# A two-layer decoder trunk: Relu and square of the MLP's partial sums emitted later than the sum, transposes spaced by bank

## The chip, the core and the metric

The kernel runs on one core of a Trainium2 chip. Five engines work side by side, each through its own list of instructions: TensorE (PE in the profile, with its weight loads as PEld), VectorE (DVE), ScalarE (ACT), GpSimd (POOL) and SyncE (SP, which here only issues transfers). The metric is the device time of one execution in microseconds (us); less is better.

## The reference

One sequence of 256 tokens with 1024 features passes two layers. Each adds a mixer (retention in layer 0, block attention in layer 1) and then an MLP, both between RMS norms. All is float32.

```
def sq_relu_mlp(x, w_up, w_down):
    h = jax.nn.relu(x @ w_up)
    return (h * h) @ w_down
...
    for i in range(DEPTH):
        pre, post, w_in, w_out, mpre, mpost, w_up, w_down = layers[i]
        h = h + rms_norm(mixers[i % N_MIXERS](rms_norm(h, pre), w_in, w_out), post)
        h = h + rms_norm(sq_relu_mlp(rms_norm(h, mpre), w_up, w_down), mpost)
```

`w_up` is 1024 x 4096 and `w_down` 4096 x 1024 in each layer; `w_in` is 1024 x 6144 in layer 0 and 1024 x 3072 in layer 1.

## The kernel before

**Numbers in two halves.** Every operand of a matmul is split into a high half in a faster float format and the rest: ScalarE copies it to `whi` (L181), VectorE subtracts to get `wlo` (L182), and TensorE makes three matmuls for each product, high x high (L238), high x low and low x high (L239, L240). Activations go the same way (L257 and L258, called `split`, tiles `act` and `qkT`). So each weight tile of 128 x 1024 costs one ScalarE instruction, one VectorE instruction and its transfer.

**The stream of weights.** `Stream` loads the weights through SP into four buffers `raw` and, for `w_up`, into four larger tiles `quad`, and turns them into `whi` and `wlo`, of which there are ten. When the next tile is split is decided as the program is written out: `Flow.now` is a clock in us that each matmul moves on by a fixed amount, and `Stream.split` may not come again before `next_t`, which it moves on by a `cost` (L172 to L176). The same clock orders the rest: a step written as a generator (`flow.spawn`) goes on when the delay that it yielded is over. These numbers only fix the order of each engine's list; on the chip the engines wait for one another by semaphores.

**The up projection.** The 4096 hidden features are eight groups of 512, and the 256 tokens two tiles `t` of 128. Groups 0 and 1 are made plainly (`in_groups_skewed`). Groups 2 to 7 come in three blocks of two groups, in a 2 x 2 scheme with seven products of half size where eight would be plain (`up_blocks`). The weight sums of the scheme are made in place in the `quad` tiles, by VectorE (L187) or by a transfer that GpSimd issues and that adds (L191). The products accumulate in three PSUM tiles, `px`, `py` and `pz`. After each product `down()` makes one step of the down projection of the two groups before (`dn`), so that TensorE goes back and forth between them. A block ends in four partial sums, each of which is squared:

- the first `pz` plus `u3` (group g+1, tile 1), after the second `py` product;
- `px` alone (group g, tile 0);
- `py` plus `p1` (group g, tile 1);
- the last `pz` plus `u2` (group g+1, tile 0), at the end of the block.

`squared` (L473) adds on VectorE (`c`, L479), applies Relu on ScalarE (L480, or L477 where nothing is added) and squares on ScalarE (L481). `turned` (L465) then waits its delay and has TensorE transpose `c` with four 128 x 128 transposes into a PSUM tile `tp_u`, which `split` brings to the hidden tile `act` for the down projection of the next block.

**PSUM.** `px`, `py`, `pz` and the transposes' tiles come from a pool of four banks. In layer 1 the last accumulator of the down projection (`dn_4961` in the order) holds one of the four, so three are left.

**The mixers.** In layer 1 `prep` copies a sum of q or k (`yq`, ScalarE), rotates it on GpSimd (`ropea`, `yq`, L860 to L865), waits its delay and has it transposed (`tp_q`). In layer 0 the first head's scores (`sd`, L740) are split to `sds` and used by the matmuls `o`.

Of the kernel before, what the change touches and what calls it, by code (L numbers as in the profile page):

```python
# [13 lines left out]
AF = mybir.ActivationFunctionType  # L14
# [3 lines left out]
P = 128  # L18
# [85 lines left out]
class Stream:  # L104
# [57 lines left out]
    def split(self, pres=(None,)):  # L162
        nc = self.nc
        while self.loaded() is None:
            assert self.load()
        op = self.order.pop(0)
        hi = self.pool.tile([P, CH], F32R, tag="whi", name="whi", bufs=self.slots)
        lo = self.pool.tile([P, CH], F32R, tag="wlo", name="wlo", bufs=self.slots)
        full = len(self.ready) >= (6 if self.quads else 4)
        if op is None:  # L170
            raw = self.raw.pop(0)[0]
            cost = (1.5 if self.quads else 2.0) if full else 1.2  # L172
        else:
            raw = self.quads[op.q][:, op.half, :]
            cost = 1.5 if full else 1.2
        n = len(pres)  # L176
        for i, pre in enumerate(pres):
            c = slice(i * CH // n, (i + 1) * CH // n)
            if pre:
                pre()  # L180
            nc.scalar.activation(hi[:, c], raw[:, c], AF.Copy)  # L181
            nc.vector.tensor_sub(lo[:, c], raw[:, c], hi[:, c].bitcast(F32))  # L182
        if op is not None:
            for q, add, name in op.sums:
                o, a = self.quads[q][:, op.half, :], self.quads[add][:, op.half, :]
                if name[1] in ("u1", "u2"):
                    nc.vector.tensor_add(o, o, a)  # L187
                    cost += 1.1
                    self.landed[name] = 0.0
                else:  # L190
                    nc.gpsimd.dma_start(o, a, accum_op=ALU.add)  # L191
                    self.dma_t = max(self.dma_t, self.flow.now) + 2.8
                    self.landed[name] = self.flow.now + 7.0
        self.live += 1
        self.quad_ops += op is not None
        self.ready.append(Chunk(hi, lo, CH * S if op is None else CH * P))
        self.next_t = max(self.next_t, self.flow.now) + cost
        while len(self.raw) < self.raws and self.load():
            pass
# [23 lines left out]
def body(ctx, tc, xT, x, gT, gpost, w_in_0, w_out_0, w_up_0, w_down_0, w_in_1, w_out_1, w_up_1, w_down_1,  # L223
# [50 lines left out]
    def new_e2(shape, name):  # L274
        return work.tile(shape, F32, tag="e2", name=name, bufs=6)
# [160 lines left out]
    def in_groups_skewed(hT, then, ready=None):  # L436

        held = []
        hT.ready(0)
        for g in range(2):  # L440
            held.append([])
            o = new_acc("ip")
            for c in range(4):
                held[g].append(ws.get())
                in_tile(hT, held[g][c], c, 0, o)
            then(g, 0, o)
        hT.ready(1)
        if ready:
            ready()
        for g in range(2):  # L450
            o = new_acc("ip")
            for c in range(4):
                in_tile(hT, held[g][c], c, 1, o)
            then(g, 1, o)


    def mlp(hT, gain, nxt, gi, qpool):
# [4 lines left out]
        def new_hid(g):  # L462
            hid[g] = new_act().rearrange("p (u j s) -> p u j s", u=2, j=4)

        def turned(g, t, c, delay):  # L465

            yield delay
            tp = new_ps([P, 4, P], "tp_u")
            turn4(tp, c)
            ts = slice(t * P, (t + 1) * P)  # L470
            split(hid[g][:, 0, :, ts], hid[g][:, 1, :, ts], tp)

        def squared(g, t, o, add=None, sign=1.0, delay=4.6):  # L473

            c = new_e2([P, 512], "c")
            if add is None:
                nc.scalar.activation(c, o, AF.Relu, scale=sign)  # L477
            else:
                nc.vector.tensor_add(c, o, add)  # L479
                nc.scalar.activation(c, c, AF.Relu, scale=sign)  # L480
            nc.scalar.activation(c, c, AF.Square)  # L481
            done[g].append(flow.spawn(turned(g, t, c, delay)))

        s_hi, s_lo = [p.tile([P, 4, 4, P], F32R, name=n, tag="act" if p is act else n)
                      for p, n in ((act, "s_hi"), (qpool, "s_lo"))]
# [33 lines left out]
        def up_blocks(g, down):  # L519


            x = new_ps([P, 512], "px")
            product(x, quad(0, 0), True)
            p1 = new_e2([P, 512], "p1")
            nc.scalar.activation(p1, x, AF.Copy)
            down()
            flow.finish(*sums)
            z = new_ps([P, 512], "pz")
            product(z, hsum(0), True)
            down()  # L530
            y = new_ps([P, 512], "py")
            product(y, hsum(1), True)
            u2 = new_e2([P, 512], "u2")
            nc.vector.tensor_add(u2, y, p1)
            down()
            product(y, hsum(2), False)
            u3 = new_e2([P, 512], "u3")
            nc.vector.tensor_add(u3, y, p1)
            squared(g + 1, 1, z, u3, -1.0, 8.0)
            down()  # L540
            product(x, quad(0, 1), False)
            squared(g, 0, x)
            down()
            product(y, quad(1, 1), False)
            squared(g, 1, y, p1)
            down()
            product(z, hsum(3), False)
            squared(g + 1, 0, z, u2, -1.0)
            down()
            down()  # L550

        def lhs(k, t):
# [4 lines left out]
        new_hid(0)  # L557
        new_hid(1)
        sums = []
        in_groups_skewed(hT, lambda g, t, o: squared(g, t, o, delay=3.6),  # L560
                         lambda: sums.append(flow.spawn(block_sums(), 1.0)))
        gb = load_gain(gain)
        rs2 = []
# [282 lines left out]
    def prep(qk, u, t, ps, wait):  # L846

        scale = hT.rs[t]
        if u == 0:
            if rsq[t] is None:  # L850
                rsq[t] = small_t("rsq")
                nc.gpsimd.tensor_scalar(rsq[t], hT.rs[t], float(MDH) ** -0.5, None, op0=ALU.mult)
            scale = rsq[t]
        y = new_e2([P, HH, MDH], "yq")
        nc.scalar.activation(y.rearrange("p h d -> p (h d)"), ps, AF.Copy, scale=scale)
        a = new_e2([P, 4, HH, 16], "ropea")
        cosb = cr[:, 0, t, None, :].to_broadcast([P, HH, 16])
        sinb = cr[:, 1, t, None, :].to_broadcast([P, HH, 16])
        x1, x2 = y[:, :, 0:16], y[:, :, 16:32]
        nc.gpsimd.tensor_mul(a[:, 0], x1, cosb)  # L860
        nc.gpsimd.tensor_mul(a[:, 1], x2, sinb)
        nc.gpsimd.tensor_mul(a[:, 2], x2, cosb)
        nc.gpsimd.tensor_mul(a[:, 3], x1, sinb)
        nc.gpsimd.tensor_sub(x1, a[:, 0], a[:, 1])
        nc.gpsimd.tensor_add(x2, a[:, 2], a[:, 3])  # L865
        yield wait
        tp = new_ps([P, HH, P], "tp_q")
        turn4(tp, y.rearrange("p h d -> p (h d)"))
        ts = slice(t * P, (t + 1) * P)
        split(qk[:, 0, :, ts], qk[:, 1, :, ts], tp)  # L870
# [112 lines left out]
    v, pts, rsq = [None, None], [], [None, None]  # L983
    qk = [new_qk(u) for u in range(2)]
    pq = []
    in_groups_skewed(hT, lambda g, t, o: pq.append(flow.spawn(prep(qk[g], g, t, o, 4.4))))
    gb = load_gain(2)
    first = flow.spawn(heads0(qk, pq))
    qk1 = [new_act().rearrange("p (a h s) -> p a h s", a=2, h=HH) for u in range(2)]
# [117 lines left out]
```

## Time and profile before

| | |
|---|---|
| time, median of 3 runs | 697.04 us (696.73 to 697.16) |
| time of the profiled execution | 697.66 us |
| its span, first to last instruction | 695.9 us |
| TensorE busy | 672.2 us, 97% of the span |
| VectorE busy | 492.6 us, 71% |
| ScalarE busy | 408.9 us, 59% |
| GpSimd busy | 101.6 us, 15% |
| read from memory | 123.39 MB, 179 GB/s over the span |

Busy is the time in which an engine has at least one instruction running. Matmuls overlap, and the profile models their ends. A time such as 275.46 is us from the start of the span. A bracket such as [3.38 <-ACT c L481] at the end of a row says how long the engine stood idle ahead of it, and which instruction ended that wait.

### The profile page before, as it was taken

What the parts mean: (1) busy time and instruction counts of PE and PEld (TensorE: products, weight loads), DVE (VectorE), ACT (ScalarE), POOL (GpSimd) and SP (SyncE); (2) the same over time, 40 slices, a digit from 0 to 9 for tenths busy, and PEclk for the clock granted to TensorE, in tenths of its full rate; (3) what the DMA queues carried; (4) which work ended last, traced back from release to release, by engine and by line L of the source; (5) the groups of instructions that cost most, each with busy time, mean ns of one, the idle gap of its engine ahead of it and who ended that gap; (6) DMA issues with size and microseconds to landing.
All of it is one profiled execution on the core that took longest, in us unless ns stands there. A gap on an engine that the chain in (4) does not pass through costs nothing.

```text
span 695.9 us, 9115 instructions
## 1 busy us (share of the span) xinstructions
PE 672.2 (97%) x3367; PEld 563.9 (81%) x3367; DVE 492.6 (71%) x595; ACT 408.9 (59%) x575; POOL 101.6 (15%) x162
## 2 busy tenths in 40 slices
PE   8999999999999998998999999999999989989996
PEld 6879898988888886786888878888888868878885
DVE  5578765666466978877866867776669777778643
ACT  6476645446355855755575657665558557555741
POOL 0122120211001100101100163912011000001001
PEclk9999999999999999999999999999999999999998
DMA  8767645464737597695647557533375976856411
GB/s 274 278 211 269 223 151 190 156 208 151 240 126 302 129 350 217 172 331 129 181 152 243 175 161 259 178 122 122 142 289 138 345 215 168 334 123 182 152 61 61
DMA packets 39645, 137.62 MB, mean 198 GB/s; under 512 B 4656, under 2 KB 5168, under 8 KB 39600
## 3 DMA queue, kind: packets, MB, share of 16 engines
q1 hardware_dynamic: 36144, 124.45, 51.1%
q0 software_dynamic: 3456, 12.58, 10.3%
q8 instruction: 26, 0.43, 0.2%
q14 instruction: 19, 0.16, 0.1%
HBM read 123.39 MB, written 1.05 MB: 179 GB/s over the span
## 4 chain that ended last, share of the span: by engine, by line
PE 69%; DVE 12%; ACT 8%; issue 5%; POOL 3%; DMA 2%; SPq 0%; POOLq 0%; DVEq 0%; ACTq 0%
PE ip L238 7%; PE ip L240 7%; PE ip L239 7%; DVE wlo L182 6%; PE dn L240 5%; PE dn L239 5%; PE dn L238 5%; ACT whi L181 4%; PE out L238 3%; PE out L240 3%; PE out L239 3%; PE qk L238 2%; PE qk L240 2%; PE qk L239 2%; DMA quad<-quad 1%
## 5 line engine op out<-in xcount | busy, mean ns | idle before, releaser
L182 DVE TENSOR_TENSOR wlo<-raw,whi 128x1024 fp32r<-128x1024 f32 (+1 forms) x179 | 213.6, 1207 | 86.1 <-ACT whi L181 78.1
L181 ACT ACTIVATE whi<-raw 128x1024 fp32r<-128x1024 f32 (+1 forms) x179 | 182.1, 1037 | 33.7 <-PE out L240 10.9
L182 DVE TENSOR_TENSOR wlo<-quad,whi 128x1024 fp32r<-128x1024 f32 x84 | 100.2, 1219 | 23.1 <-ACT whi L181 23.1
L238 PE MATMUL ip<-whi,act 128*128 128x512 f32 x288 | 114.2, 397 | 0.0
L239 PE MATMUL ip<-wlo,act 128*128 128x512 f32 x288 | 112.5, 390 | 0.2 <-DVE wlo L182 0.2
L240 PE MATMUL ip<-whi,act 128*128 128x512 f32 x288 | 112.4, 390 | 0.0
L238 PE MATMUL dn<-whi,act 128*128 128x512 f32 (+1 forms) x288 | 106.5, 370 | 0.0
L240 PE MATMUL dn<-whi,act 128*128 128x512 f32 (+1 forms) x288 | 105.6, 367 | 0.0
L239 PE MATMUL dn<-wlo,act 128*128 128x512 f32 (+1 forms) x288 | 105.3, 366 | 0.0
L181 ACT ACTIVATE whi<-quad 128x1024 fp32r<-128x1024 f32 x84 | 86.4, 1049 | 21.8 <-DMA quad<-quad 15.2
L240 PEld LDWEIGHTS ip<-whi,act 128*128 128x128 f32 x288 | 54.1, 188 | 11.6
L239 PEld LDWEIGHTS ip<-wlo,act 128*128 128x128 f32 x288 | 54.2, 188 | 10.7 <-DVE wlo L182 0.7
L238 PEld LDWEIGHTS ip<-whi,act 128*128 128x128 f32 x288 | 54.1, 188 | 10.0
L240 PEld LDWEIGHTS dn<-whi,act 128*128 128x128 f32 x288 | 54.2, 188 | 9.8 <-DVE act L258 0.9
L239 PEld LDWEIGHTS dn<-wlo,act 128*128 128x128 f32 x288 | 54.3, 188 | 9.4
L238 PEld LDWEIGHTS dn<-whi,act 128*128 128x128 f32 x288 | 54.3, 188 | 9.2
L191 POOL DMA_DIRECT2D quad<-quad x24 | 21.2, 882 | 206.2 <-DVE quad L187 100.2
L480 ACT ACTIVATE c<-c 128x512 f32<-128x512 f32 x18 | 11.4, 632 | 66.9 <-DVE c L479 66.9
L238 PE MATMUL qk<-act,whi 128*128 128x256 f32 x128 | 37.8, 296 | 1.4 <-ACT whi L181 1.4
L238 PE MATMUL out<-whi,act 128*128 128x512 f32 x96 | 37.8, 394 | 0.0
L240 PE MATMUL qk<-act,wlo 128*128 128x256 f32 x128 | 37.6, 293 | 0.0
L240 PE MATMUL out<-whi,act 128*128 128x512 f32 x96 | 37.4, 390 | 0.0
(187 smaller groups left out, 1116.1 us busy)
## 6 DMA issues: line engine op xcount, KB each, us to landing
raw<-in_w_in SPq DMA_DIRECT2D x69, 512.0 KB, 4.4
raw<-in_w_down SPq DMA_DIRECT2D x64, 512.0 KB, 5.0
quad<-in_w_up SPq DMA_DIRECT2D x48, 512.0 KB, 7.7
raw<-in_w_out SPq DMA_DIRECT2D x24, 512.0 KB, 3.4
quad<-quad POOLq DMA_DIRECT2D x24, 512.0 KB, 5.4
raw<-in_w_up SPq DMA_DIRECT2D x16, 512.0 KB, 3.6
gb<-in_gpost SPq DMA_DIRECT2D x4, 512.0 KB, 7.9
raw<-in_w_in SPq DMA_DIRECT2D x6, 256.0 KB, 5.9
```

The source lines that it names most:

```text
L181: nc.scalar.activation(hi[:, c], raw[:, c], AF.Copy)
L182: nc.vector.tensor_sub(lo[:, c], raw[:, c], hi[:, c].bitcast(F32))
L191: nc.gpsimd.dma_start(o, a, accum_op=ALU.add)
L238: nc.tensor.matmul(o, a[0], b[0], start=first, stop=False, skip_group_check=again)
L239: nc.tensor.matmul(o, a[0], b[1], start=False, stop=False, skip_group_check=again)
L240: nc.tensor.matmul(o, a[1], b[0], start=False, stop=last, skip_group_check=again)
L480: nc.scalar.activation(c, c, AF.Relu, scale=sign)
```

## The change

`turned` and `squared` become one generator. It allocates `c`, adds where there is something to add, and then yields 2.2 us of the program's clock before it writes out Relu and square; where there is nothing to add, Relu and square follow at once, as they did. The delays ahead of the transposes are new: 4.0 instead of 4.6, to which the 2.2 come, for the third and the fourth sum, 6.0 instead of 8.0 plus the 2.2 for the first, 6.5 instead of 4.6 for the sum without an add. The first two groups keep 3.6. The first four transposes of q and k wait 5.6 instead of 4.4. And the `cost` of a split outside the up projection is 1.3 instead of 1.2 while few tiles are ready.

```diff
@@ -169,7 +169,7 @@
-            cost = (1.5 if self.quads else 2.0) if full else 1.2
+            cost = (1.5 if full else 1.2) if self.quads else (2.0 if full else 1.3)
@@ -462,24 +462,23 @@
-        def turned(g, t, c, delay):
-
+        def squared(g, t, o, add=None, sign=1.0, delay=4.0):
+
+            c = new_e2([P, 512], "c")
+            if add is not None:
+                nc.vector.tensor_add(c, o, add)
+                yield 2.2
+                o = c
+            nc.scalar.activation(c, o, AF.Relu, scale=sign)
+            nc.scalar.activation(c, c, AF.Square)
             yield delay
             tp = new_ps([P, 4, P], "tp_u")
             turn4(tp, c)
             ts = slice(t * P, (t + 1) * P)
             split(hid[g][:, 0, :, ts], hid[g][:, 1, :, ts], tp)
 
-        def squared(g, t, o, add=None, sign=1.0, delay=4.6):
-
-            c = new_e2([P, 512], "c")
-            if add is None:
-                nc.scalar.activation(c, o, AF.Relu, scale=sign)
-            else:
-                nc.vector.tensor_add(c, o, add)
-                nc.scalar.activation(c, c, AF.Relu, scale=sign)
-            nc.scalar.activation(c, c, AF.Square)
-            done[g].append(flow.spawn(turned(g, t, c, delay)))
+        def square(g, *args):
+            done[g].append(flow.spawn(squared(g, *args)))
@@ -536,16 +535,16 @@
-            squared(g + 1, 1, z, u3, -1.0, 8.0)
+            square(g + 1, 1, z, u3, -1.0, 6.0)
...
-            squared(g, 0, x)
+            square(g, 0, x, None, 1.0, 6.5)
...
-            squared(g, 1, y, p1)
+            square(g, 1, y, p1)
...
-            squared(g + 1, 0, z, u2, -1.0)
+            square(g + 1, 0, z, u2, -1.0)
@@ -983,7 +982,7 @@
-    in_groups_skewed(hT, lambda g, t, o: pq.append(flow.spawn(prep(qk[g], g, t, o, 4.4))))
+    in_groups_skewed(hT, lambda g, t, o: pq.append(flow.spawn(prep(qk[g], g, t, o, 5.6))))
```

The next rows are ScalarE's list in the first block of layer 0, from around the first sum to the Relu of the third (`py`); `c<-c` is a Relu after an add or a square, `c<-px` the Relu of the sum without an add. Before:

```order
L480 ACTIVATE c<-c 128x512
L481 ACTIVATE c<-c 128x512
L181 ACTIVATE whi<-raw 128x1024
L181 ACTIVATE whi<-quad_2031 128x1024 x2
L477 ACTIVATE c<-px 128x512
L481 ACTIVATE c<-c 128x512
L181 ACTIVATE whi<-raw 128x1024 x2
L257 ACTIVATE act<-tp_u 128x4x128
L181 ACTIVATE whi<-quad_2030 128x1024
L257 ACTIVATE act<-tp_u 128x4x128
L480 ACTIVATE c<-c 128x512
L481 ACTIVATE c<-c 128x512
```

The same place in the changed kernel:

```order
L181 ACTIVATE whi<-raw 128x1024
L181 ACTIVATE whi<-quad_2031 128x1024
L472 ACTIVATE c<-c 128x512
L473 ACTIVATE c<-c 128x512
L181 ACTIVATE whi<-quad_2031 128x1024
L472 ACTIVATE c<-px 128x512
L473 ACTIVATE c<-c 128x512
L181 ACTIVATE whi<-raw 128x1024 x2
L257 ACTIVATE act<-tp_u 128x4x128
L181 ACTIVATE whi<-quad_2030 128x1024
L257 ACTIVATE act<-tp_u 128x4x128
L181 ACTIVATE whi<-quad_2030 128x1024
```

Two weight tiles now stand ahead of the first sum's Relu, and one more ahead of the third's, which follows right behind the last row.

VectorE's list at the same place, from the first `act` to the add of the last sum (`c<-pz`). Before:

```order
L258 TENSOR_TENSOR act<-tp_u,act 128x4x128
L182 TENSOR_TENSOR wlo<-quad_2030,whi 128x1024
L187 TENSOR_TENSOR quad_2030<-quad_2030,quad_2032 128x1024
L258 TENSOR_TENSOR act<-tp_u,act 128x4x128
L479 TENSOR_TENSOR c<-py,p_2300 128x512
L182 TENSOR_TENSOR wlo<-quad_2030,whi 128x1024
L187 TENSOR_TENSOR quad_2030<-quad_2030,quad_2032 128x1024
L182 TENSOR_TENSOR wlo<-raw,whi 128x1024
L182 TENSOR_TENSOR wlo<-quad_2030,whi 128x1024
L187 TENSOR_TENSOR quad_2030<-quad_2030,quad_2029 128x1024
L258 TENSOR_TENSOR act<-tp_u,act 128x4x128
L479 TENSOR_TENSOR c<-pz,u_2389 128x512
```

In the changed kernel:

```order
L258 TENSOR_TENSOR act<-tp_u,act 128x4x128
L182 TENSOR_TENSOR wlo<-quad_2030,whi 128x1024
L187 TENSOR_TENSOR quad_2030<-quad_2030,quad_2032 128x1024
L469 TENSOR_TENSOR c<-py,p_2300 128x512
L258 TENSOR_TENSOR act<-tp_u,act 128x4x128
L182 TENSOR_TENSOR wlo<-quad_2030,whi 128x1024
L187 TENSOR_TENSOR quad_2030<-quad_2030,quad_2032 128x1024
L182 TENSOR_TENSOR wlo<-raw,whi 128x1024
L182 TENSOR_TENSOR wlo<-quad_2030,whi 128x1024
L187 TENSOR_TENSOR quad_2030<-quad_2030,quad_2029 128x1024
L469 TENSOR_TENSOR c<-pz,u_2389 128x512
L258 TENSOR_TENSOR act<-tp_u,act 128x4x128
```

Each of the two adds has moved ahead of the `act` that stood in front of it; nothing else has moved.

On TensorE, in the first block of layer 1, the second and the fourth group of transposes, as pieces of the difference (the second leaves the `py` product and comes six matmuls into `dn`; the fourth leaves the end of `dn` and comes six matmuls into the next `px`):

```order
 L240 MATMUL py<-whi,act 128x512
-L262 MATMUL tp_u<-ident,c 128x128 x4
 L238 MATMUL py<-whi,act 128x512
...
 L240 MATMUL dn<-whi,act 128x512
+L262 MATMUL tp_u<-ident,c 128x128 x4
 L238 MATMUL dn<-whi,act 128x512
...
 L240 MATMUL dn<-whi,act 128x256
-L262 MATMUL tp_u<-ident,c 128x128 x4
 L238 MATMUL dn_4961<-whi,act 128x256
...
 L240 MATMUL px<-whi,act 128x512
+L262 MATMUL tp_u<-ident,c 128x128 x4
 L238 MATMUL px<-whi,act 128x512
```

In layer 0 the four stand in the changed kernel six matmuls into `py`, six into the `dn` behind it, six into the `dn` behind `pz`, and six into the next `px`; before, they stood three and nine matmuls into `py`, right behind `pz`, and ahead of the next `px`. The first transposes of q stand six matmuls of `ip` later than before. SP's and GpSimd's lists are those of before, but for one `raw` load in layer 1 that now comes behind the load of a gain (`gb`).

## Rows read from the trace of the kernel before

**Rows 1.** The page's first part: busy time, share of the span and number of instructions of TensorE, its weight loads and the other engines.

```profile
PE 672.2 (97%) x3367; PEld 563.9 (81%) x3367; DVE 492.6 (71%) x595; ACT 408.9 (59%) x575; POOL 101.6 (15%) x162
```

**Rows 2.** Who waited for whom on TensorE over the whole span: us in total, times, longest.

```profile
PE tp_u L262 <- ACT c L481: 9.9, 4, 3.4
PE tp_u L262 <- DVE act L258: 1.7, 1, 1.7
```

**Rows 3.** TensorE in order of time, the five longest waits: start, us, engine, line, names, shapes, and in brackets the idle time and what ended it.

```profile
279.23 1.12 PE L262 MATMUL tp_u<-ident,c 128*128 128x128 f32 x4 [3.38 <-ACT c L481]
...
325.98 0.66 PE L262 MATMUL tp_u<-ident,c 128*128 128x128 f32 x4 [2.30 <-ACT c L481]
...
560.39 0.65 PE L262 MATMUL tp_u<-ident,c 128*128 128x128 f32 x4 [1.66 <-DVE act L258]
...
574.83 0.66 PE L262 MATMUL tp_u<-ident,c 128*128 128x128 f32 x4 [1.94 <-ACT c L481]
...
622.31 0.66 PE L262 MATMUL tp_u<-ident,c 128*128 128x128 f32 x4 [2.26 <-ACT c L481]
```

**Rows 4.** Busy time in chosen stretches: the twelve matmuls of the `px` product behind four of these waits, and one stretch inside the second of them. Columns: stretch, its length, busy us and count of PE, PEld, DVE, ACT, POOL, granted TensorE clock (1.00 is full), busy share of the DMA engines and GB/s.

```profile
280.00:284.01 4.01, 4.01 (x14) 3.24 (x13) 3.82 (x4) 3.56 (x5) 0.00 (x0) 0.69 0.00 0
326.39:330.82 4.43, 4.43 (x16) 3.48 (x14) 3.88 (x4) 3.92 (x5) 0.00 (x0) 0.61 0.01 4
575.68:580.03 4.35, 4.35 (x15) 3.42 (x13) 4.24 (x5) 3.48 (x5) 0.00 (x0) 0.61 0.00 0
623.16:625.90 2.74, 2.74 (x15) 2.26 (x13) 2.62 (x3) 2.57 (x5) 0.00 (x0) 1.00 0.00 0
326.90:330.30 3.40, 3.40 (x9) 2.64 (x8) 3.36 (x3) 3.23 (x4) 0.00 (x0) 0.50 0.02 5
```

**Rows 5.** VectorE in order of time in the first block of layer 0, ahead of the first of these waits.

```profile
254.78 0.69 DVE L479 TENSOR_TENSOR c<-pz,u 128x512 f32<-128x512 f32 x1
257.79 1.23 DVE L182 TENSOR_TENSOR wlo<-raw,whi 128x1024 fp32r<-128x1024 f32 x1 [2.31 <-ACT whi L181]
...
264.65 1.22 DVE L182 TENSOR_TENSOR wlo<-quad,whi 128x1024 fp32r<-128x1024 f32 x1
265.90 1.23 DVE L187 TENSOR_TENSOR quad<-quad,quad 128x1024 f32<-128x1024 f32 x1
...
267.65 0.68 DVE L479 TENSOR_TENSOR c<-py,p 128x512 f32<-128x512 f32 x1
270.64 1.23 DVE L182 TENSOR_TENSOR wlo<-quad,whi 128x1024 fp32r<-128x1024 f32 x1 [2.31 <-ACT whi L181]
...
277.17 0.68 DVE L479 TENSOR_TENSOR c<-pz,u 128x512 f32<-128x512 f32 x1
```

**Rows 6.** ScalarE in order of time in the same block, and one row of the next.

```profile
251.83 1.06 ACT L181 ACTIVATE whi<-quad 128x1024 fp32r<-128x1024 f32 x1 [2.55 <-DVE wlo L182]
255.51 0.63 ACT L480 ACTIVATE c<-c 128x512 f32<-128x512 f32 x1 [2.62 <-DVE c L479]
...
256.71 1.05 ACT L181 ACTIVATE whi<-raw 128x1024 fp32r<-128x1024 f32 x1
...
259.56 0.58 ACT L477 ACTIVATE c<-px 128x512 f32<-128x512 f32 x1
...
260.70 2.00 ACT L181 ACTIVATE whi<-raw 128x1024 fp32r<-128x1024 f32 x2
...
268.36 0.63 ACT L480 ACTIVATE c<-c 128x512 f32<-128x512 f32 x1 [3.75 <-DVE c L479]
...
277.89 0.63 ACT L480 ACTIVATE c<-c 128x512 f32<-128x512 f32 x1 [4.90 <-DVE c L479]
...
295.63 1.06 ACT L181 ACTIVATE whi<-quad 128x1024 fp32r<-128x1024 f32 x1 [2.19 <-DMA quad<-quad]
```

**Rows 7.** TensorE in order of time in the same block: the start of the second `px` product, the first transposes and the matmul behind them, the last matmul of `pz`.

```profile
255.16 0.39 PE L238 MATMUL px<-whi,act 128*128 128x512 f32 x1
...
261.28 0.60 PE L262 MATMUL tp_u<-ident,c 128*128 128x128 f32 x4
261.64 0.48 PE L238 MATMUL py<-whi,act 128*128 128x512 f32 x1
...
269.48 0.39 PE L240 MATMUL pz<-whi,s_lo 128*128 128x512 f32 x1
```

**Rows 8.** The first block of layer 1: TensorE's first transposes, and VectorE's step that empties their bank.

```profile
556.74 0.60 PE L262 MATMUL tp_u<-ident,c 128*128 128x128 f32 x4
...
559.65 0.68 DVE L258 TENSOR_TENSOR act<-tp_u,act 128x512 fp32r<-128x512 f32 x1
```

**Rows 9.** TensorE at the first transposes of q in layer 1.

```profile
405.19 0.66 PE L262 MATMUL tp_q<-ident,yq 128*128 128x128 f32 x4 [0.99 <-POOL yq L865]
```

**Rows 10.** Layer 0, the first head: VectorE ahead of the scores, and TensorE at the matmuls that use them.

```profile
39.77 4.63 DVE L182 TENSOR_TENSOR wlo<-raw,whi 128x1024 fp32r<-128x1024 f32 x4
44.32 0.68 DVE L740 TENSOR_TENSOR sd<-st,dT_sb 128x512 f32<-128x512 f32 x1
...
45.72 0.50 PE L238 MATMUL o<-v,sds 128*128 128x512 f32 x1 [0.52 <-ACT sds L257]
```

**Rows 11.** Busy time from the first wait to the second, one block of layer 0, and in its middle part; columns as in rows 4.

```profile
275.46:323.29 47.83, 44.45 (x197) 36.52 (x196) 37.08 (x36) 28.87 (x35) 3.51 (x4) 0.96 0.77 223
284.00:323.00 39.00, 39.00 (x179) 32.30 (x178) 30.59 (x30) 23.23 (x28) 3.51 (x4) 1.00 0.83 249
```

More of the change, by code (lines that the diff above doesn't have):

```diff
@@ L559, in mlp @@
         sums = []
-        in_groups_skewed(hT, lambda g, t, o: squared(g, t, o, delay=3.6),
+        in_groups_skewed(hT, lambda g, t, o: square(g, t, o, None, 1.0, 3.6),
                          lambda: sums.append(flow.spawn(block_sums(), 1.0)))
```

## The prediction

> **What bounds the kernel now.** First the page's engine times [rows 1]: TensorE is busy for 672.2 of 695.9 us, nothing else for more than 71%. So a change to ScalarE's and VectorE's order can only pay where TensorE waits for them, and 23.7 us seem to be all that is left. Next, who TensorE waited for [rows 2]: by far the most is `tp_u`, the transposes of the squared sums, 9.9 us in four waits for ScalarE's square and 1.7 us in one for VectorE. The order of time gives the places [rows 3]: the end of the first and of the second block of each layer (279.23, 325.98, 574.83, 622.31), and the second transposes in the first block of layer 1 (560.39). The third blocks have none. The reader should see that the same four transposes come round six times and that only certain ones are late.
>
> A wait costs more than its bracket. Matmuls of 512 columns last 0.39 us but follow each other every 0.227 us (twelve in 2.74 us, fourth row of [rows 4]), so a bracket counts from the end of a matmul that would have been overlapped for 0.16 us. The losses are therefore 3.38, 2.30, 1.66, 1.94 and 2.26 plus 0.16 each: 3.54 + 2.46 + 1.82 + 2.10 + 2.42 = 12.34 us.
>
> Then the stretches behind the waits [rows 4]. The twelve `px` matmuls take 4.01, 4.43 and 4.35 us behind three of the waits and 2.74 behind the fourth. The granted clock shows why: 0.69, 0.61 and 0.61 against 1.00, and 0.50, which is 1.2 GHz, inside the second stretch. TensorE had stood idle just before. The slow stretches cost 1.27 + 1.69 + 1.61 = 4.57 us, and they are hidden in TensorE's busy time: PE is busy for the whole of each. The wait of 2.26 us was not followed by one, so not every wait pays this.
>
> The Trainium skill says that matmul busy time is no good measure of how near a kernel is to its roof (Perfetto Trace Analysis, Identifying the Most-Contended Engine). The trace agrees, as the 4.57 us just named are all busy; by idle time alone the sum below would be 4.57 us smaller.
>
> **Why the squares are late.** VectorE and ScalarE wait for each other in turns. In the first block of layer 0 ScalarE reaches the Relu of a sum before VectorE has added it, and stands for 2.62, 3.75 and 4.90 us [rows 6]. The next weight split is queued behind that Relu, so VectorE, once it has added, has nothing to subtract and stands for 2.31 us, at 257.79 and at 270.64 [rows 5]. What it lost there it is late with at the next add: `pz` is done at 269.48 + 0.39 = 269.87 [rows 7], yet its sum is added at 277.17, and squared at about 279.2, where TensorE waits.
>
> **The change, part by part.** No compute instruction is added or removed, and transfers are the same; all is order.
>
> *Relu 2.2 us behind the add.* ScalarE now splits two weight tiles before the first Relu and one more before the third, so VectorE has work while it would have stood. I follow the first block of layer 0 with durations of the rows, from the start of `px` at 255.16 [rows 7]. TensorE: twelve `px`, twelve `dn`, six `py` (30 x 0.227) bring the first transposes to 261.96; they take 0.36 (261.28 to 261.64) and end, by their own row, 0.60 after their start. Twelve matmuls on, the second stand at 265.04; then six `dn`, `pz` and six `dn` to the third at 270.84, then 18 `dn` and six `px` to the fourth at 276.64.
>
> ScalarE: `px` is done at 258.04; Relu 0.58 and square 0.63 to 259.3; two raw splits (2.00) to 261.3; `act` of the first transposes (ready at 262.56, taken as long as a Relu) to 263.1; a split (0.95 to the next) to 264.1; `act` of the second (ready 265.64) to 266.2; a split to 267.2. VectorE follows: `wlo` 264.2 to 265.35, its weight sum to 266.6 (1.14 to 1.25 each [rows 5]), add of `py` to 267.3, where it was 267.65 to 268.33; then `act` 0.6, `wlo`, weight sum, `wlo`, `wlo`, weight sum: 0.6 + 5 x 1.17 brings the add of `pz` to about 273.7 to 274.4, where it was 277.17. Most of the 3.4 us are the 2.31 us of standing, the 0.6 of an `act` that now comes behind the add, and 0.35 kept from the add before. Relu and square (0.66 each) make it ready at 275.75. TensorE asks at 276.64, later than before by its own six matmuls of `px`. The slack is 0.9 us, so the wait of 3.54 us goes. The third transposes are ready by 267.3 + 1.3 = 268.6 and wanted at 270.84.
>
> The second block has the same list from `px` on, so the same slack. In layer 1 half-width matmuls of `dn_4961` lie between, and the fourth is wanted some 1.4 us later by the program's own count (12 half matmuls), so its slack is above 2 us. Saved: 3.54 + 2.46 + 2.10 + 2.42 = 10.52 us, and the three slow stretches, 4.57 us.
>
> Two tiles ahead of the first Relu could delay it. Its add ends at 255.47 [rows 5]; ScalarE is free from 251.83 + 1.06 = 252.89 [rows 6], and two splits of 0.95 end at 254.8, so the Relu starts at 255.5 as before. It costs nothing as long as the tiles have landed; if they had landed only when they were split before, at 256.71 and 257.66, the square would be ready near 260.1, still 1.9 us ahead of 261.96.
>
> What is late next? VectorE has 37.1 us of work in a block of 47.8 [rows 11]; with 5.2 us gone it is 37.1 of 42.6, 87%. It fits. The first `wlo` of the next block's weights is done at 265.35 and used from 275.3, ten us ahead, so a split that slips behind an `act` is covered; without that cover each would cost 1.14.
>
> *Transposes spaced by bank.* In layer 1 the second transposes waited until VectorE had emptied the bank of the first: first at 556.74, `act` from 559.65 to 560.33 [rows 8], second at 560.39. The bank is still the same one, but now 15 matmuls lie between, 0.36 + 15 x 0.227 = 3.77 us where 3.59 are needed. As `act` too now comes earlier (VectorE does not stand before it), 1.82 us are saved. In the two later blocks this wait was too short to count.
>
> Here a rule of the Trainium skill speaks against the change: independent matmul groups should rotate through different PSUM banks, so that one is emptied while the next is filled (Perfetto Trace Analysis, Optimizing Tensor Performance, Matmuls). The trace has such a wait, the 1.66 us above; by the rule spacing alone would not do, and the sum would be 1.8 us smaller.
>
> *First q and k transposes later.* TensorE waited 0.99 us for GpSimd's rotation [rows 9], a loss of 1.15. Six more matmuls (1.36) go ahead of it: 1.15 us saved, with 0.2 to spare.
>
> *Cost 1.3.* In the first head one weight split moves from ahead of the scores to behind them: three of the four `wlo` (4.63 us [rows 10]) stay, `sd` comes 1.14 earlier, and the wait of 0.52 (0.68 lost) goes. The moved tile is the fourth of a row of which TensorE uses one per 2.7 us, so it is not missed. Elsewhere splits change places with single instructions where TensorE did not wait; I take nothing, between plus and minus 0.5.
>
> **Sum.** 10.52 + 4.57 + 1.82 + 1.15 + 0.68 = 18.7 us. The profiled execution took 697.66, so it would take 678.9. The median of the runs is 0.62 below that execution, which makes **678.3 us**.
>
> **Rivals.**
> *A rest stays in layer 0* (0.20). The slack of 0.9 us there is small against a chain of ten instructions. One split more in it (1.14 + 0.95 = 2.1) leaves a wait of 1.2 in two blocks, 2.4 us; if the clock falls too, as it did behind waits of 1.94 and 2.30, 1.3 to 1.7 more each. That gives 680.7 to 684.
> *The bank still holds* (0.05). One more `wlo` of 1.14 ahead of `act` makes the 3.77 us too short by 1 in three blocks: 681.3. For it speaks the rule above, against it that VectorE's standing goes.
> *Weights become the limit* (0.08). In the busy middle of a block VectorE ran at 30.59 of 39.0 us, 78% [rows 11]. If it cannot do better than that over a whole block, a block lasts 37.1 / 0.78 = 47.5 and the four blocks gain almost nothing: about 694.5; at 83% a block is 44.7 and the time near 686. Against it: the idle time is the standing that the change removes.
> *The deferred Relu starves* (0.04), which ends slower. If the tile now ahead of the first Relu lands late, Relu and transposes wait with it, as a split did for 2.19 us on an adding transfer [rows 6]. The first square has 261.96 - 256.8 = 5.1 us to spare, so with a delay w six blocks lose 6 x (w - 5.1) plus a slow stretch of 1.5 each. It outweighs 18.7 us from w = 6.7; at 8 it would be 704.7. The rows bound w by 3.8 (252.89 to 256.71), hence the low chance.
> *The waits only move* (0.03): 696 to 697.
> The remaining 0.60 is the forecast, 676 to 681.
>
> **How the numbers follow.** The likeliest is 678.3. Down to 675.8 reach the 0.5 us taken as nothing above and small gaps that no term holds; up to 686 are the first two rivals and the milder third, so 0.85 to 0.88 lies inside. 0.2% is 1.4 us, about what a measurement here can tell from no change. Faster 0.92, the same 0.04, slower 0.04.
>
> **What would show it.** Right: no wait of TensorE for `tp_u` above 1 us, granted clock 1.00 from the first block to the end of the second MLP, ScalarE's waits for `c` well under the 2.6 to 4.9 us, VectorE's 2.31 us rows gone, `tp_q` and `o` without a bracket. Wrong: a wait at the fourth transposes of layer 0 (first rival), at the second of layer 1 (second), brackets that name `wlo` or `whi` before `dn`, `px`, `py` or `pz` (third), or at the first transposes of a block (fourth).

## The result and the profile after

The changed kernel takes **677.33 us** (median of 4 runs, 676.14 to 677.89) against 696.88 (4 runs, 696.31 to 697.16): a ratio of 0.9718, 95% interval 0.9701 to 0.9735, and 19.6 us less. Forecast were 678.3 us, between 675.8 and 686.0, with 0.92 for faster. Its profiled execution took 676.89 us.

The page's engine times. They answer to [rows 1]:

```profile
PE 663.8 (98%) x3367; PEld 560.1 (83%) x3367; DVE 492.4 (73%) x595; ACT 409.5 (61%) x575; POOL 103.6 (15%) x162
```

VectorE and ScalarE do what they did (492.4 and 409.5 us; before 492.6 and 408.9). TensorE is busy for 8.4 us less with the same 3367 matmuls, of which 4.57 are the slow stretches of [rows 4]: a gain that no idle time shows.

Who TensorE waited for, the whole list (total us, times, longest). It answers to [rows 2]:

```profile
PE qk L238 <- ACT whi L181: 1.6, 1, 1.6
PE warm L289 <- DVE junk L284: 1.2, 1, 1.2
PE qk L240 <- DVE wlo L182: 0.4, 2, 0.2
PE tp_q L262 <- POOL yq L864: 0.4, 1, 0.4
PE ip L239 <- DVE wlo L182: 0.3, 1, 0.3
PE st L240 <- DVE qkT L258: 0.2, 1, 0.2
```

The reader is to see what is missing: `tp_u`, 11.6 us before, is not in it. `tp_q` keeps 0.4 us, at another place than [rows 9] (440.84, the last of its transposes), and `o` [rows 10] is gone. The other rows are of the start-up and of the first head, all before 41 us.

Busy time in stretches: first the matmuls behind the fourth transposes of the first block of layer 0 and of layer 1, which answer to [rows 4], then one block of layer 0 from the start of one second `px` product to the next, which answers to [rows 11] (columns as there):

```profile
275.82:278.55 2.73, 2.73 (x14) 2.23 (x13) 2.69 (x3) 2.55 (x5) 0.00 (x0) 1.00 0.00 0
...
560.92:563.65 2.73, 2.73 (x14) 2.23 (x13) 2.73 (x3) 2.56 (x5) 0.00 (x0) 1.00 0.00 0
...
253.51:296.20 42.69, 42.69 (x197) 35.35 (x196) 37.24 (x38) 29.83 (x37) 3.47 (x4) 1.00 0.86 271
```

The granted clock is 1.00, and so it is behind those of the second blocks; the only half-clock stretches of this execution lie in the start-up (3.41 us from 9.10) and at the very end (from 671.28). The block lasts 42.69 us where it lasted 47.83, TensorE runs through all of it, and VectorE's 37.24 us are now 87% of it.

The first block of layer 0 in order of time, as in [rows 5 to 7]. TensorE, with the start of `px`, the four transposes and, in the last row, the matmul behind them:

```profile
253.51 0.39 PE L238 MATMUL px<-whi,act 128*128 128x512 f32 x1
...
260.31 0.60 PE L262 MATMUL tp_u<-ident,c 128*128 128x128 f32 x4
...
263.51 0.60 PE L262 MATMUL tp_u<-ident,c 128*128 128x128 f32 x4
...
269.44 0.60 PE L262 MATMUL tp_u<-ident,c 128*128 128x128 f32 x4
...
275.36 0.60 PE L262 MATMUL tp_u<-ident,c 128*128 128x128 f32 x4
275.71 0.48 PE L238 MATMUL px<-whi,act 128*128 128x512 f32 x1
```

ScalarE, with the Relu of the first, third and fourth sum and the last square:

```profile
253.80 0.63 ACT L472 ACTIVATE c<-c 128x512 f32<-128x512 f32 x1 [0.72 <-DVE c L469]
...
265.65 0.63 ACT L472 ACTIVATE c<-c 128x512 f32<-128x512 f32 x1
...
272.77 0.63 ACT L472 ACTIVATE c<-c 128x512 f32<-128x512 f32 x1 [2.10 <-DVE c L469]
273.44 0.63 ACT L473 ACTIVATE c<-c 128x512 f32<-128x512 f32 x1
```

VectorE, with the three adds, what follows the first two, and the split behind the block's end:

```profile
253.08 0.69 DVE L469 TENSOR_TENSOR c<-pz,u 128x512 f32<-128x512 f32 x1
253.69 1.22 DVE L182 TENSOR_TENSOR wlo<-raw,whi 128x1024 fp32r<-128x1024 f32 x1
...
264.93 0.69 DVE L469 TENSOR_TENSOR c<-py,p 128x512 f32<-128x512 f32 x1
265.53 0.68 DVE L258 TENSOR_TENSOR act<-tp_u,act 128x512 fp32r<-128x512 f32 x1
...
272.05 0.68 DVE L469 TENSOR_TENSOR c<-pz,u 128x512 f32<-128x512 f32 x1
...
275.05 1.23 DVE L182 TENSOR_TENSOR wlo<-quad,whi 128x1024 fp32r<-128x1024 f32 x1 [1.72 <-ACT whi L181]
```

The three waits of ScalarE for a sum, 2.62, 3.75 and 4.90 us [rows 6], are 0.72, none and 2.10. VectorE goes from the add straight to its next work where it stood for 2.31 [rows 5]; only the last such place is left, with 1.72, and it no longer matters: the square ends at 273.44 + 0.63 = 274.07, and TensorE comes for it at 275.36, 1.29 us later.

### The profile page after: what moved, and what is told of

The parts are those of the page before. It is cut to its first block, busy times and chain, and to the rows that moved or that the text cites. A ratio compares the mean times of both kernels' runs of the same rounds, so it can differ in the third digit from the quotient of the medians.

```text
span 675.1 us, 9117 instructions
## 1 busy us (share of the span) xinstructions
PE 663.8 (98%) x3367; PEld 560.1 (83%) x3367; DVE 492.4 (73%) x595; ACT 409.5 (61%) x575; POOL 103.6 (15%) x162
## 4 chain that ended last, share of the span: by engine, by line
PE 89%; issue 3%; DVE 2%; POOL 2%; ACT 1%; DMA 1%; SPq 0%; POOLq 0%; DVEq 0%; ACTq 0%
PE dn L240 8%; PE dn L238 8%; PE dn L239 8%; PE ip L239 8%; PE ip L240 8%; PE ip L238 8%; PE out L240 3%; PE out L238 3%; PE out L239 3%; PE py L238 2%; PE py L239 2%; PE py L240 2%; PE qk L240 2%; PE qk L238 2%; PE qk L239 2%
## 5 line engine op out<-in xcount | busy, mean ns | idle before, releaser
L182 DVE TENSOR_TENSOR wlo<-quad,whi 128x1024 fp32r<-128x1024 f32 x84 | 101.1, 1222 | 12.5 <-ACT whi L181 12.2
L240 PEld LDWEIGHTS ip<-whi,act 128*128 128x128 f32 x288 | 54.1, 188 | 11.6
L239 PE MATMUL out<-wlo,act 128*128 128x512 f32 x96 | 37.4, 389 | 0.0
```

The source lines that it names most:

```text
L239: nc.tensor.matmul(o, a[0], b[1], start=False, stop=False, skip_group_check=again)
L240: nc.tensor.matmul(o, a[1], b[0], start=False, stop=last, skip_group_check=again)
```

## The experiments

**The deferred Relu alone, and the spacing alone.** In the first, the transposes keep the places of the kernel before (the delays are cut by what the Relu is deferred); in the second the Relu follows its add at once, and the transposes stand where the changed kernel has them. One group is an exception: the first transposes of each block of layer 0 stand three matmuls later with the Relu alone, as in the changed kernel, and where they were with the spacing alone. Their square is ready more than 4 us ahead in both old and new kernel (256.80 against 261.28 before), so nothing waits there. Neither kernel has the new `cost` or the later q and k. First `relu_alone`, against the changed kernel:

```diff
-        def squared(g, t, o, add=None, sign=1.0, delay=4.0):
+        def squared(g, t, o, add=None, sign=1.0, delay=2.4):
...
-            square(g + 1, 1, z, u3, -1.0, 6.0)
+            square(g + 1, 1, z, u3, -1.0, 5.8)
...
-            square(g, 0, x, None, 1.0, 6.5)
+            square(g, 0, x, None, 1.0, 4.6)
```

> The kernel before with the deferred Relu alone: 2.2 us between a sum's add and its Relu, the transposes at the places of the kernel before, the first q and k transposes and the costs as before. My theory (the late squares come from ScalarE and VectorE standing for each other): nearly all of the 15 us of layer 0's and layer 1's fourth transposes goes; as the fourth transposes are asked six matmuls (1.36 us) earlier than in the changed kernel, where the square was 1.29 us early in layer 0 and 1.82 in layer 1, a wait of 0 to 0.3 us is left in two or three places; the bank wait of layer 1 shrinks to 0 to 0.5 us per block, the waits for yq (1.15) and for the first head's sds (0.68) stay. 679 to 682 us. The rival (the spacing alone does it: later transposes simply stop asking too early) expects most of the waits to stay: 690 us or more, with tp_u waits of 2 us at the fourth transposes.

Then `spacing_alone`, against the kernel before:

```diff
-        def squared(g, t, o, add=None, sign=1.0, delay=4.6):
+        def squared(g, t, o, add=None, sign=1.0, delay=6.2):
...
-            squared(g + 1, 1, z, u3, -1.0, 8.0)
+            squared(g + 1, 1, z, u3, -1.0, 8.2)
...
-            squared(g, 0, x)
+            squared(g, 0, x, None, 1.0, 6.5)
```

> The kernel before with the spacing alone: the Relu right behind its add as before, the transposes at the places of the changed kernel, the first q and k transposes and the costs as before. My theory: the squares stay as late as before, so the fourth transposes, asked 1.36 us later in layer 0 and some 1.4 to 1.8 us later in layer 1, lose 3.54, 2.46, 2.10 and 2.42 less that, about 4 us together instead of 10.5; the bank wait in layer 1 (1.82) goes; half-clock stretches of 1.3 to 1.7 us go behind the shorter waits and may stay behind the longest. 685 to 689 us. The rival (the spacing does it all) expects 679 to 681 and no wait for tp_u.

Measured: the Relu alone 681.94 us (681.08 to 682.42; ratio 0.9789, 0.9760 to 0.9818, to the 696.40 of the kernel before that was measured beside it), the spacing alone 683.87 (683.45 to 684.36; 0.9819, 0.9796 to 0.9843). That is 14.5 and 12.5 us, 27 if they added, where both in one kernel give 17.0 (below). They repair the same waits, and the spacing does more by itself than the theory had (685 to 689) and less than its rival (679 to 681).

TensorE in the kernel with the Relu alone, at the fourth transposes of the first block of layer 0 and at the first two of layer 1, then who it waited for:

```profile
276.39 0.66 PE L262 MATMUL tp_u<-ident,c 128*128 128x128 f32 x4 [0.61 <-ACT c L473]
...
549.01 0.60 PE L262 MATMUL tp_u<-ident,c 128*128 128x128 f32 x4
...
551.03 0.66 PE L262 MATMUL tp_u<-ident,c 128*128 128x128 f32 x4
```

```profile
PE tp_u L262 <- ACT c L473: 1.2, 2, 0.6
```

The time is at the upper end of what was expected (679 to 682). Of the waits for late squares two of 0.6 us are left, where 0 to 0.3 were expected. The second transposes of layer 1 follow the first by 2.02 us with no bracket, where they waited 1.66 [rows 3]: the bank is free in time although the transposes stand as close as they did.

The kernel with the spacing alone, same block of layer 0, first TensorE:

```profile
278.86 0.66 PE L262 MATMUL tp_u<-ident,c 128*128 128x128 f32 x4 [1.35 <-ACT c L481]
279.27 0.48 PE L238 MATMUL px<-whi,act 128*128 128x512 f32 x1
279.59 0.39 PE L239 MATMUL px<-wlo,act 128*128 128x512 f32 x1
```

Who TensorE waited for at `tp_u` over its whole span:

```profile
PE tp_u L262 <- ACT c L481: 2.9, 3, 1.4
```

VectorE in the same block:

```profile
258.13 1.23 DVE L182 TENSOR_TENSOR wlo<-raw,whi 128x1024 fp32r<-128x1024 f32 x1 [2.31 <-ACT whi L181]
...
269.92 0.69 DVE L258 TENSOR_TENSOR act<-tp_u,act 128x512 fp32r<-128x512 f32 x1 [1.85 <-ACT act L257]
...
276.80 0.68 DVE L479 TENSOR_TENSOR c<-pz,u 128x512 f32<-128x512 f32 x1
279.32 0.69 DVE L258 TENSOR_TENSOR act<-tp_u,act 128x512 fp32r<-128x512 f32 x1 [1.84 <-ACT act L257]
```

VectorE still stands behind each add, as the theory has it, but the time is under the 685 to 689 that it gave. The later second transposes take their `act` out of the way of the `py` add, and VectorE then stands for 1.85 instead of 2.31. The wait shrinks from 3.38 to 1.35, by 2.0 and not only by the 1.36 of the six matmuls; in the second blocks it shrinks from 2.30 and 2.26 to 0.19 and 0.12, in the first block of layer 1 only from 1.94 to 1.36. And none of the waits that are left is followed by a slow stretch: behind the 1.35 the matmuls come 0.23 to 0.32 us apart. So the theory was right that both parts are needed for no wait at all, and wrong on how much the lesser one leaves: a little on the waits (about 4 us at the four late squares, where 3.0 are left), and more on the clock, as it reckoned with slow stretches and none is left.

**The MLP part alone, and what is not of the MLP.** The changed kernel without its `cost` and its later q and k (`mlp_alone`); the kernel before with those two alone (`qk_and_cost_alone`), and with the `cost` alone (`cost_alone`). The lines of the last two, of which the second has only the first pair:

```diff
-            cost = (1.5 if self.quads else 2.0) if full else 1.2
+            cost = (1.5 if full else 1.2) if self.quads else (2.0 if full else 1.3)
...
-    in_groups_skewed(hT, lambda g, t, o: pq.append(flow.spawn(prep(qk[g], g, t, o, 4.4))))
+    in_groups_skewed(hT, lambda g, t, o: pq.append(flow.spawn(prep(qk[g], g, t, o, 5.6))))
```

> The changed kernel without its q and k placing and without the cost of 1.3: the MLP part alone. If the parts add, it is 1.8 to 2.1 us slower than the changed kernel: 679.2 to 679.5. If the two small parts are worth nothing it stays at 677.3.

> The kernel before with only the first q and k transposes six matmuls later and the cost of a quarter split at 1.3: the wait for yq (1.15) and the first head's wait for sds (0.68) go, nothing else moves: 1.8 us faster, 695.0. By a rival (such waits are refilled by the next one) it is the same within 0.5 us: 696.4 to 697.4.

> The kernel before with only the cost of a quarter split at 1.3. Together with the later q and k transposes it gave 2.9 us, where 1.15 and 0.68 were expected. If the rest comes from the cost, this kernel gains 1.7 us: 694.7. If it gives the first head's wait alone, 0.7 us: 695.7. If the start-up, which was 1 us shorter in the two profiled executions with this cost, is only the execution's own scatter, its profile shows the second wait of TensorE for the first weights again (0.5 to 1.1 us).

Measured: the MLP part alone 679.45 us (679.10 to 679.83; ratio 0.9756, 0.9733 to 0.9779), 17.0 below the 696.40 beside it and 2.1 above the changed kernel, as expected if the parts add. The changed kernel had its own measurement of the kernel before beside it (696.88) and was 19.6 below that, so by the two differences the small parts are worth 2.6. The other two alone 693.54 (691.78 to 693.81; 0.9951, 0.9935 to 0.9967), 2.9 us better and not 1.8. The `cost` alone 696.17 against 697.37 (0.9988, 0.9967 to 1.0010): 1.2 us, with an interval that holds 0.7 and nothing as well as 1.7.

Part of the 2.9 is probably chance. In the profiles of ten kernels whose lists are the same so far, the first `ip` matmul starts between 19.95 us (with q, k and `cost`) and 21.95, and what differs is when the first weights land. That the start-up has nothing to do with the `cost` is not shown, though: the six kernels with it start `ip` at 19.95 to 21.13, the four without it at 21.33 to 21.95. The profile of the `cost` alone shows the second wait for the first weights again:

```profile
7.90 0.39 PE L238 MATMUL qk<-act,whi 128*128 128x256 f32 x1 [0.67 <-ACT whi L181]
```

Another part is the clock. These two kernels have the late squares of the kernel before, and the stretches behind them differ from one execution to the next. Behind the same four waits as in [rows 4], first with q, k and `cost`, then with the `cost` alone:

```profile
278.09:282.09 4.00, 4.00 (x12) 3.13 (x11) 3.81 (x4) 3.56 (x5) 0.00 (x0) 0.50 0.00 0
325.78:330.20 4.42, 4.42 (x22) 3.65 (x21) 3.87 (x4) 4.25 (x6) 0.00 (x0) 1.00 0.01 4
571.87:576.20 4.33, 4.33 (x22) 3.59 (x21) 4.21 (x5) 4.16 (x7) 0.00 (x0) 1.00 0.00 0
617.70:620.44 2.74, 2.74 (x9) 2.17 (x8) 2.63 (x3) 2.56 (x5) 0.00 (x0) 0.54 0.00 0
```

```profile
278.36:282.38 4.02, 4.02 (x13) 3.17 (x12) 3.83 (x4) 3.56 (x5) 0.00 (x0) 0.63 0.00 0
324.82:329.20 4.38, 4.38 (x15) 3.47 (x14) 3.83 (x4) 3.92 (x5) 0.00 (x0) 0.61 0.02 4
574.63:579.00 4.37, 4.37 (x15) 3.47 (x14) 4.26 (x5) 3.48 (x5) 0.00 (x0) 0.61 0.00 0
622.08:624.80 2.72, 2.72 (x10) 2.15 (x9) 2.61 (x3) 2.55 (x5) 0.00 (x0) 0.61 0.00 0
```

After waits of nearly the same length (3.4, 2.3, 1.9 and 2.3 us) the clock fell behind the first three before, behind the first and the last here, and behind all four in the last kernel. What the two small edits give apart from these draws can be read from the profiles, where a stretch holds the same matmuls in every kernel.

- From the first `ip` matmul to the last `o` matmul of the first head it takes 26.45 us before (21.49 to 47.94) and 25.41 in the changed kernel (21.01 to 46.42). All six kernels with the new `cost` lie between 25.37 and 25.42, the other three without it between 26.42 and 26.45. So the `cost` gives 1.0 us in the first head, where 0.68 was expected.
- Around the transposes of q and k, from the `ip` matmul at 403.81 to the one at 460.00 of the kernel before, it takes 56.19 us. The five kernels with both edits need 54.86 to 54.92, 1.3 us less, where 1.15 was expected; the kernel with the `cost` alone needs 0.35 us more.

Both together give 2.3 to 2.4 us, and the `cost` alone 0.7. What the medians show beyond that is left to the start-up, the clock and scatter.

**More work on VectorE.** The add of each block's last sum is written three or six times in a row, with the same result.

```diff
-                nc.vector.tensor_add(c, o, add)
+                for _ in range(n):
+                    nc.vector.tensor_add(c, o, add)
...
-            square(g + 1, 0, z, u2, -1.0)
+            square(g + 1, 0, z, u2, -1.0, 4.0, 3)
```

> The changed kernel with the add of each block's last sum written three times in a row, the result unchanged: some 1.2 us more on VectorE, ahead of the fourth square, in six blocks. My theory: the slack of 1.29 us in the first two blocks of layer 0, and of 1.8 in layer 1, takes it: no wait for tp_u above 0.1, 677.3 to 678. Rival (VectorE sets the pace of a block): 6 x 1.2 = 7 us, 684.

> As the last, with the add written six times, the result unchanged: some 3.0 us more on VectorE. My theory: the slack is used up and the rest is waited: 1.7 us in the first two blocks of layer 0, 1.2 in those of layer 1, nothing in the third blocks, where 2.65 and 3.5 us are to spare, with 0.16 to each wait 6.4 us together; half-clock stretches of 1.3 to 1.7 us behind none to four of them: 683.5 to 689. Rival (VectorE sets the pace): 6 x 3.0, 695.

Measured: 677.83 us (677.10 to 678.07; ratio 0.9719, 0.9689 to 0.9749) with three, 688.17 (687.09 to 689.34; 0.9871, 0.9833 to 0.9910) with six. VectorE's adds in the first block, with three and with six, and TensorE's fourth transposes there, with three and with six:

```profile
272.19 2.13 DVE L470 TENSOR_TENSOR c<-pz,u 128x512 f32<-128x512 f32 x3
```

```profile
272.22 4.31 DVE L470 TENSOR_TENSOR c<-pz,u 128x512 f32<-128x512 f32 x6
```

```profile
275.26 0.39 PE L240 MATMUL px<-whi,act 128*128 128x512 f32 x1
275.71 0.66 PE L262 MATMUL tp_u<-ident,c 128*128 128x128 f32 x4
```

```profile
277.91 0.66 PE L262 MATMUL tp_u<-ident,c 128*128 128x128 f32 x4 [2.23 <-ACT c L474]
```

An add costs 0.72 us here (2.13 / 3), more than the 0.60 that I reckoned with. Two more are 1.44, and the slack of 1.29 is used up: the fourth transposes start 0.45 us after the last matmul ahead of them instead of 0.23. Five more are 3.6, and 3.6 less 1.29 is 2.3, measured 2.23. So the slack is what the rows say, and VectorE's work is free up to it: with 7.8 us more of busy VectorE (500.2 against 492.4) the median is 0.5 us higher, which is within the scatter of both kernels and about what these 0.22 us come to in the first two blocks of layer 0. With six the four waits are 2.23, 2.22, 1.71 and 1.71, with 0.16 each and 0.35 in a fifth 8.9 us. Stretches behind the first two of them:

```profile
278.40:282.80 4.40, 4.40 (x15) 3.46 (x14) 3.93 (x4) 4.23 (x6) 0.00 (x0) 0.61 0.00 0
325.10:328.00 2.90, 2.90 (x15) 2.40 (x14) 2.38 (x3) 2.83 (x4) 0.00 (x0) 1.00 0.02 6
```

As many matmuls take 4.40 us behind the first and 2.90 behind the second, after waits that differ by 0.01 us. With those 1.5 the sum is 10.4 of the 10.8 us by which the medians differ.

**A Relu deferred further.** 4.0 us instead of 2.2, the transposes where they are (the first of each block of layer 1 come three matmuls later).

```diff
-        def squared(g, t, o, add=None, sign=1.0, delay=4.0):
+        def squared(g, t, o, add=None, sign=1.0, delay=2.2):
...
-                yield 2.2
+                yield 4.0
...
-            square(g + 1, 1, z, u3, -1.0, 6.0)
+            square(g + 1, 1, z, u3, -1.0, 4.2)
```

> The changed kernel with 4.0 instead of 2.2 us between add and Relu, the transposes where they are: about one more weight split stands ahead of each Relu. My theory: the squares had 1.29 to 6.6 us to spare and VectorE stands less, so nothing waits: 677.3 plus or minus 0.5. Rival (the deferred Relu starves): the fourth squares come a split later (0.95) with their slack of 1.29 gone and first ones with tiles not landed; waits for tp_u of up to 1 us in four to six blocks: 680 to 683.

Measured: 676.75 us (676.41 to 678.04; ratio 0.9709, 0.9678 to 0.9740), not to be told from the changed kernel, and no wait for `tp_u`. The fourth square of the first block is ready 1.29 us ahead as before, since its Relu still waits for the add and not for the split in front of it:

```profile
272.35 0.63 ACT L472 ACTIVATE c<-c 128x512 f32<-128x512 f32 x1 [1.15 <-DVE c L469]
```

So 2.2 us is no fine point: the Relu stood 2.10 us idle before its add came, and another split (0.95) fits in there; 1.15 are left.

## Why the prediction was right, point by point

**The late squares (10.52 us and 1.82).** Right, and close to its own steps. Counted from the start of `px`, the add of `py` was put at 11.4 to 12.1 us (266.6 to 267.3, less 255.16) and runs from 11.4 to 12.1 (264.93 to 265.62, less 253.51); that of the last sum was put at 18.5 to 19.2 and runs from 18.5 to 19.2, where it started at 22.0. The last square was put at 20.59 and is ready at 20.56. The slack at the fourth transposes was put at 0.9 and is 1.29, nearly all of the difference because TensorE comes later than reckoned: three groups of transposes cost 0.48 us each (260.31 to 263.51 holds one group and twelve matmuls, 3.20 us) and not 0.36. At the third it was put at 2.2 and is 2.49. In layer 1 it was put above 2 and is 1.82, and there the reason was wrong: the fourth transposes come 22.05 us behind the start of `px` (538.41 to 560.46), only 0.2 later than in layer 0 and not 1.4, because the half-width matmuls stand in the place of full ones; the square is ready 0.3 earlier. The first sum's Relu starts 0.29 us after `px` begins, as it did (0.35), so the two tiles ahead of it delayed nothing. VectorE's share of a block was put at 87% and is 87%. That this chain is the cause is shown by the runs: with the Relu alone and the fourth transposes where they were the waits fall to two of 0.6, and work put back on VectorE brings them back by the amount that exceeds the slack.

**How the two parts share it.** This step was incomplete. The prediction gave the squares to the Relu, with 1.36 us of later asking, and the bank to the spacing. Alone, the spacing takes 2.0 and 2.1 us off the waits in layer 0, since it also moves an `act` out of the way; and the bank's wait goes with the Relu alone too, with the transposes 2.02 us apart. The sum came out all the same because it holds each wait once, whichever part removes it.

**The bank as a rival.** In the changed kernel VectorE's step that empties the bank starts 1.27 us after the first transposes, where it took 2.91 [rows 8] (TensorE puts those at 544.61):

```profile
545.88 0.69 DVE L258 TENSOR_TENSOR act<-tp_u,act 128x512 fp32r<-128x512 f32 x1
```

It is done 1.9 us ahead of the second transposes (548.48), which still write the same bank: the only other one about to come free is that of `py`, whose add starts at 549.23. The Trainium skill says that independent matmul groups should rotate through different PSUM banks (Perfetto Trace Analysis, Optimizing Tensor Performance, Matmuls). By that rule the wait would have stayed; the trace shows it gone with one bank, once the engine that empties it was not held up. Whether a further bank would have done as well was not run.

**The slow stretches (4.57 us).** Right in what the change does: the granted clock is 1.00 behind all four. The size holds for the one execution that was read; the same waits gave two to four such stretches elsewhere. The 4.57 was a draw, and the term ought to have had a range of its own. It was also a little small: the first stretch began with the transposes, which took 0.77 us up to the next matmul (279.23 to 280.00 in [rows 3] and [rows 4]) where those of the second block took 0.41, and the sum counted only the `px` matmuls.

**q and k, and the first head (1.15 and 0.68).** Both waits are gone. Together with `cost` they measured 2.1 us (changed kernel against its MLP part alone) to 2.9 (against the kernel before), where 1.83 was forecast; the stretches above give 2.3 to 2.4.

**What no term held.** The profiled execution came out at 676.89, not 678.9. The start-up took 0.48 us less in it (first `ip` matmul at 21.01, before at 21.49), which is within what the ten profiles show and no part of the mechanism. Of the other 1.5 us the two small edits hold 0.5 and the transposes at half clock 0.36. Some 0.6 more lie at places in layer 1 where the prediction saw no wait or one too short to count: the second transposes of the two later blocks, which stood 0.42 us behind the matmul ahead of them instead of 0.23, and the fourth of the third block. So it was partly luck that the median came within 1 us of 678.3: an execution with two or four slow stretches would have shifted the gain by 1.3 to 1.7 us. Of the rivals, the one that a rest stays in layer 0 would have been right without the later fourth transposes: the Relu alone leaves its two waits there, 0.6 where 1.2 was priced. VectorE as the limit is refuted by the block itself, which runs at the 87% that this rival held to be out of reach, and by the adds written three times; the 686 that it gives for 83% does not follow from its own 44.7 us either (four blocks of 3.1 us and 1.83 make about 683). The starving Relu is refuted up to 4.0 us of deferral. The waits did not move: the list of the changed kernel has no new one but the 0.4 us at `tp_q`.

## What to carry to other kernels

When two engines each wait for the other in turns, look at what is queued behind the instruction that waits: a Relu placed right behind the add that it needs keeps the next split from the engine that is to add next, and moving it one or two splits later gave back 14.5 us with no work removed, some 5 of them slow stretches that no longer followed the waits. Measure the slack at the place where the bottleneck asks, by adding work until a wait appears; it tells how far the engine beside it may still be loaded. Two edits that repair the same wait don't add, so take each alone before giving either its share.

## What the runs showed of the hardware

Waits of TensorE of 1.9 to 2.3 us were followed by 3.4 us at half clock (1.2 instead of 2.4 GHz) in some executions and not in others: seven of eleven such waits ahead of `tp_u`, in all profiles together, were, all three of 3.4, and none of the four of 1.7 or the shorter ones. In the start-up shorter waits can be followed by one: six of the ten profiles, that of the changed kernel among them, have 3.41 us at half clock from 7.7 to 9.1 us on, behind waits of at most 1.6 us. What decides between them no run here shows. The kernel before, which has such waits, scatters from 693.56 to 699.87 us over 13 runs on one chip; the kernels whose waits stay under 1.4 us scatter by 0.7 to 1.8 us over 4 runs each, but so did the kernel before in the 4 runs beside the changed kernel (0.85 us). That the clock makes a difference is argued from it, not shown: the mean clock and the time of its runs go together only loosely.
